# Giving every matmul operand the same place within 256 bytes, and the expert queries without transposes

## The chip, the cores and the metric

The kernel runs on one core of one Trainium2 chip. The metric is the device time of one execution in microseconds (us): the median of three runs, and one further execution taken by the hardware profiler, from which the rows below come. Lower is better.

## What is computed

Two transformer blocks follow each other on 256 tokens of width 2048, all in float32. The first has a retention layer (8 heads, 256 wide) and a latent attention layer, each between a modulated norm and a gated residual. The second has a mixed attention layer (16 "forgetting" heads, 16 "dilated" heads) and a layer of experts: each token scores 8 x 2 x 128 keys, takes the 16 best pairs of each head out of 128 x 128 experts, and sums the chosen experts.

```
def peer(x, w_query, sub_keys, expert_down, expert_up):
    q = (xt @ w_query).reshape(T, PEER_HEADS, 2, PEER_HALF)
    scores = jnp.einsum('thpc,hpnc->thpn', q, sub_keys)
    vals, idx = lax.top_k(scores, PEER_TOPK)
    ...
    u = jnp.take(expert_down, ec, axis=0)
    hdn = jax.nn.gelu(jnp.einsum('ted,td->te', u, xc))
    ...
    return jnp.einsum('te,ted->td', gc * hdn, vsel)
```

## The kernel before, in words

**Split products.** Every large product is made of three matmuls on operands that are split into a high and a low part (`split`, lines 171 to 173: ScalarE copies `raw` to `wh`, VectorE forms `wl = raw - wh`). A matmul has a stationary operand of 128 x 128, which TensorE loads (the rows PEld), and a moving one, which it streams past it, 256 to 512 columns. The load for the next matmul starts with the stream of the present one, so two reads of SBUF run beside each other: the stream of matmul n and the weights of matmul n+1.

**Three shapes** carry the time.

- *Tokens stationary, weights moving* (`proj_steps`, lines 243 to 245): the activations' columns (`hT`, `zT`, `mT`, `zT1`) are stationary, 512 columns of `wh` or `wl` move (384, 416 or 424 in the latent layer; 256 and 272 in the two blocks with the forget gates).
- *Weights stationary, tokens moving* (`turned_steps`, lines 271 to 273, for the retention's queries and keys; `hidden`, lines 1214 to 1216, for the experts' first product): 128 columns of `wh` or `wl` are stationary, the 256 tokens of `hT` move. The result has its dimensions on the partitions.
- *Experts' second product* (`up_steps`, lines 1294 to 1296): the gated hidden values `Wh`, `Wl` are stationary, 512 columns of `wh` or `wl` move.

**Places in SBUF.** Pools lie one behind the other, in the order in which they are opened, and tiles behind each other in a pool. Nothing rounds their addresses, so small tiles (`colv` 928 bytes, `mhalf` 32 bytes, ...) shift all that lies behind. Of the address in the built program, the remainder by 256 bytes (the "place" below) is the same for all buffers of a kind:

| operands of a matmul n and of the load for n+1 | stream at | weights at | stream minus weights, by 256 |
|---|---|---|---|
| `proj`, weights `hT`, `zT1` (512 columns) | 224 | 32 | 192 |
| `proj`, weights `mT` | 224 | 64 | 160 |
| `proj`, weights `zT` | 224 | 96 | 128 |
| `proj`, 424 columns, odd rows of the block | 128 | 32 | 96 |
| `proj`, 256 columns (forget block) | 224 | 32 | 192 |
| `turned`, `hidden` (256 columns) | 32 | 224 | 64 |
| `up` (512 columns) | 224 | 224 | 0 |

**The experts' queries** (`scores`, from line 1360): four blocks of 512 columns of `peer_query_2` go through `proj`, 96 matmuls of 512 columns each. Per block, ScalarE copies the two results out of PSUM with the factor `rtok` (line 1396); `tail` then, as a background task of the next block, transposes 2 x 4 squares of 128 x 128 (line 1374), copies them (1376), multiplies by the keys (1380) and copies the scores (1382). The scores feed `route`, the search for the best, mostly VectorE work, which runs beside the queries and the first experts.

**Order.** One program order per engine, made by the builder from the code's order and its pools; background tasks are interleaved by fixed rates (`later`, `tick`). SP issues all weight transfers in that order. The constants `cst` (identity, ones, masks, tables) come by one DMA at the start and stay.

Of the kernel before, what the change touches and what calls it, by code (L numbers as in the profile page):

```python
# [32 lines left out]
HB = 4  # L33
ADA_RATE = 0.3


C_ID, C_ONE, C_TRI, C_IOTA, C_CAUSAL, C_DIL, C_COS2, C_SIN2, C_INVF, C_COLF, C_END = (
    0, 128, 256, 384, 512, 768, 1152, 1168, 1184, 1216, 1224)
# [86 lines left out]
class Net:  # L125
    def __init__(self, ctx, tc, a):
        self.ctx, self.tc, self.nc, self.a = ctx, tc, tc.nc, a
        self.keep = ctx.enter_context(tc.tile_pool(name="keep", bufs=1))
        self.st = ctx.enter_context(tc.tile_pool(name="stream", bufs=1))
        self.sm = ctx.enter_context(tc.tile_pool(name="small", bufs=1))  # L130
        self.dr = ctx.enter_context(tc.tile_pool(name="dram", bufs=1, space=bass.MemoryType.DRAM))
        self.ps = ctx.enter_context(tc.tile_pool(name="psum", bufs=1, space=PSUM))
        self.bg = []
        self.nhalf, self.extra = 0, None
        self.places = places()
# [39 lines left out]
    def weights(self, name, k, c0):  # L175
# [5 lines left out]
        for j in range(2):  # L181
            wh, wl = self.halves()
# [75 lines left out]
    def turned_steps(self, ps, hT, nk, name, c0):  # L258
# [4 lines left out]
        for k0 in range(hT[0], hT[0] + nk, 4):  # L263
            for wh, wl in self.weights(name, k0, c0):
# [122 lines left out]
    def start(self):  # L387
        nc, keep, a = self.nc, self.keep, self.a
        self.ident = keep.tile([128, 128], F32, name="ident")
        self.colv = keep.tile([128, V_END], F32, name="colv")  # L390
        nc.scalar.dma_start(self.colv, a["vectors"])
        nc.sync.dma_start(self.ident, a["consts"][:, C_ID:C_ID + 128])
        self.cst = keep.tile([128, C_END], F32, name="cst")
# [4 lines left out]
        self.mhalf = keep.tile([128, 8], F32, name="mhalf")  # L398
        nc.vector.memset(self.mhalf, -0.5)

        self.cact = keep.tile([128, 16], F32, name="cact")
# [7 lines left out]
        nc.scalar.dma_start(self.cst, a["consts"])  # L409
# [3 lines left out]
    def angles(self, pool):  # L413
# [5 lines left out]
        self.cos = keep.tile([128, 2, 32], F32, name="cos")  # L419
        self.sin = keep.tile([128, 2, 32], F32, name="sin")  # L420
# [8 lines left out]
        pi = keep.tile([128, 2], I32, name="posi")  # L429
        nc.scalar.dma_start(pi, pos.rearrange("o (b p) -> p (o b)", p=128))  # L430
        pf = keep.tile([128, 2], F32, name="posf")
# [146 lines left out]
    def retention(self):  # L578
# [3 lines left out]
        self.A1 = keep.tile([128, 16], F32, name="A1")  # L582
        self.B1 = keep.tile([128, 16], F32, name="B1")
        with self.phase("ret", 8), self.tc.tile_pool(name="ret", bufs=1) as pool:
            A = pool.tile([128, 16], F32, name="A0")
            B = pool.tile([128, 16], F32, name="B0")
# [195 lines left out]
    def latent(self):  # L782
        nc, a = self.nc, self.a
        w_in, w_out, w_uq, w_ukv = "mla_w_in", "mla_w_out", "mla_w_uq", "mla_w_ukv"
        causal = self.cst[:, C_CAUSAL:C_CAUSAL + 256]
        scale = float(192 ** -0.5)
        with self.phase("mla", 7), ExitStack() as es:
            pool = es.enter_context(self.tc.tile_pool(name="mla", bufs=1))
            G = pool.tile([128, D], F32, name="G1")
            front = ExitStack()  # L790
# [4 lines left out]
            ss = pool.tile([128, 4], F32, name="latss")  # L795
# [16 lines left out]
            def latents():  # L812

                lr = pool.tile([128, 4], F32, name="latr")
# [126 lines left out]
            fa = self.keep.tile([128, 16], F32, name="fa")  # L941
# [6 lines left out]
            self.rtok = self.keep.tile([128, 2], F32, name="rtok")  # L948
# [25 lines left out]
    def mixed(self):  # L974
        nc, a = self.nc, self.a
        w_in, w_out = "w_in_2", "w_out_2"
        causal = self.cst[:, C_CAUSAL:C_CAUSAL + 256]
        with self.phase("mix", 8), self.tc.tile_pool(name="mix", bufs=1) as pool:
            hT, rtok = self.hT, self.rtok
            next(self.norms)  # L980
            norms = self.later(self.norms, 0.9)
            trig = pool.tile([128, 2, 2, 8], F32, name="trig")
# [3 lines left out]
            lf = pool.tile([128, 2, 16], F32, name="lf")  # L986
# [20 lines left out]
            cum = pool.tile([128, 2, 16], F32, name="cum")  # L1007
# [12 lines left out]
            def project(n, g, beside=iter(())):  # L1020
# [17 lines left out]
                for off in (0, 1024):  # L1038
                    def ev(tb, p, off=off):
# [5 lines left out]
                        dst = pool.tile([128, 1, 8, 66], F32, name="qk2", bufs=2)  # L1045
# [26 lines left out]
            def head(n, g, h):  # L1072
# [3 lines left out]
                else:  # L1076
                    mask = lambda tb: self.cst[:, C_DIL:C_DIL + 128] if tb == 0 else \
                        self.cst[:, C_DIL + 128:C_DIL + 384]
# [14 lines left out]
            def finish(n):  # L1093
# [7 lines left out]
                r = pool.tile([128, 2], F32, name=f"r_{n}")  # L1101
# [38 lines left out]
            self.rtok = self.keep.tile([128, 2], F32, name="rtok2")  # L1140
# [3 lines left out]
    def peer(self):  # L1144
# [5 lines left out]
        with self.phase("peer", 4), self.tc.tile_pool(name="peer", bufs=1) as pool:  # L1150
# [30 lines left out]
            def fetch(e):  # L1181
# [4 lines left out]
                for half in range(2):  # L1186
                    dh, dl = self.halves()
# [173 lines left out]
    def scores(self, qp, rp, hT, slots, normed, fetch):  # L1361
# [8 lines left out]
        def tail(b, qn):  # L1370
            for tb in range(2):
                p2 = self.tmp()
                for j in range(4):
                    nc.tensor.transpose(p2[:, j * 128:j * 128 + 128], qn[tb][:, j * 128:j * 128 + 128], self.ident)
                qT = qn[tb]
                nc.scalar.activation(qT, p2, AF.Copy)
                yield
                p3 = self.tmp()
                for j in range(4):
                    nc.tensor.matmul(p3[:, j * 128:j * 128 + 128], qT[:, j * 128:j * 128 + 128], kT[:, b * 4 + j, :],  # L1380
                                     start=True, stop=True)
                nc.scalar.activation(sc[tb][:, b * 4:b * 4 + 4, :].rearrange("p k n -> p (k n)"), p3, AF.Copy)
# [8 lines left out]
        for b in range(4):  # L1391
            qn = []

            def ev(tb, p, qn=qn):
                qn.append(self.w())
                nc.scalar.activation(qn[tb], p, AF.Copy, scale=self.rtok[:, tb:tb + 1])
# [12 lines left out]
        return steps, tail(3, qn)  # L1409
# [215 lines left out]
```

## Time and profile before

| | us |
|---|---|
| median of the runs (lowest, highest) | 3252.47 (3251.17, 3254.47) |
| the profiled execution: its own time | 3252.83 |
| its span, first to last instruction | 3251.0 |
| TensorE busy | 3159.2 (97%) |
| weight loads (PEld) busy | 2762.0 (85%) |
| VectorE busy | 2366.0 (73%) |
| ScalarE, GpSimd busy | 1558.4, 414.4 |

The profiled execution's own time is 1.8 us more than its span, and 0.4 us more than the median. A matmul's row shows its full passage (a 512-column one about 390 ns), and passages overlap; what one adds to the time is the distance from its start to the start of the next. The timeline lists the starts to 0.01 us.

### The profile page before, as it was taken

What the parts mean: (1) busy time and instruction counts of PE and PEld (TensorE: products, weight loads), DVE (VectorE), ACT (ScalarE), POOL (GpSimd) and SP (SyncE); (2) the same over time, 40 slices, a digit from 0 to 9 for tenths busy, and PEclk for the clock granted to TensorE, in tenths of its full rate; (3) what the DMA queues carried; (4) which work ended last, traced back from release to release, by engine and by line L of the source; (5) the groups of instructions that cost most, each with busy time, mean ns of one, the idle gap of its engine ahead of it and who ended that gap; (6) DMA issues with size and microseconds to landing.
All of it is one profiled execution on the core that took longest, in us unless ns stands there. A gap on an engine that the chain in (4) does not pass through costs nothing.

```text
span 3251.0 us, 47605 instructions
## 1 busy us (share of the span) xinstructions
PE 3159.2 (97%) x18562; PEld 2762.0 (85%) x18562; DVE 2366.0 (73%) x3918; ACT 1558.4 (48%) x2162; POOL 414.4 (13%) x487
## 2 busy tenths in 40 slices
PE   4999999999999999999999999999999999999998
PEld 4888977887798888888888999999888898999987
DVE  6898878878787675455669966998766656556665
ACT  3444434344545455555554444555444444444444
POOL 0001210201000320000000312886000000000000
PEclk9999999999999999999999999999999999999999
DMA  8875677786585435444454456777966755555554
GB/s 342 305 268 203 244 270 296 254 300 243 202 289 201 143 130 196 144 153 145 143 185 152 158 198 212 260 242 258 314 238 235 239 201 207 196 202 186 194 194 142
DMA packets 141681, 705.68 MB, mean 217 GB/s; under 512 B 12680, under 2 KB 45832, under 8 KB 67728
## 3 DMA queue, kind: packets, MB, share of 16 engines
q1 hardware_dynamic: 139152, 696.51, 60.9%
q10 hardware_dynamic: 2304, 6.14, 0.5%
q8 instruction: 145, 2.38, 0.3%
q14 instruction: 80, 0.66, 0.1%
HBM read 676.38 MB, written 26.21 MB: 216 GB/s over the span
## 4 chain that ended last, share of the span: by engine, by line
PE 83%; DVE 8%; DMA 4%; issue 3%; ACT 1%; POOL 0%; SPq 0%; DVEq 0%; POOLq 0%; ACTq 0%
PE acc L244 11%; PE acc L245 11%; PE acc L243 11%; PE acc L1294 7%; PE acc L1296 7%; PE acc L1295 7%; PE tmp L1214 5%; PE tmp L1216 5%; PE tmp L1215 5%; DVE wl L173 3%; PE acc L272 2%; PE acc L273 2%; PE acc L271 2%; PE tmp L359 1%; PE acc L1214 1%
## 5 line engine op out<-in xcount | busy, mean ns | idle before, releaser
L173 DVE TENSOR_TENSOR wl<-raw,wh 128x1024 fp32r<-128x1024 f32 (+4 forms) x983 | 1197.2, 1225 | 469.9 <-ACT wh L172 467.6
L172 ACT ACTIVATE wh<-raw 128x1024 fp32r<-128x1024 f32 (+4 forms) x983 | 1018.3, 1044 | 1017.9 <-PE acc L245 343.6
L244 PE MATMUL acc<-wl,hTh 128*128 128x512 f32 (+4 forms) x1280 | 497.4, 389 | 13.1 <-DVE wl L173 13.1
L243 PE MATMUL acc<-wh,hTh 128*128 128x512 f32 (+4 forms) x1280 | 498.3, 391 | 1.5 <-ACT wh L172 1.5
L245 PE MATMUL acc<-wh,hTl 128*128 128x512 f32 (+4 forms) x1280 | 496.7, 388 | 0.0
L1214 PE MATMUL tmp<-hTh,wh 128*128 128x256 f32 x1280 | 361.5, 282 | 0.0
L1216 PE MATMUL tmp<-hTl,wh 128*128 128x256 f32 x1280 | 357.6, 279 | 0.0
L1215 PE MATMUL tmp<-hTh,wl 128*128 128x256 f32 x1280 | 357.5, 279 | 0.0
L1294 PE MATMUL acc<-wh,Wh 128*128 128x512 f32 x812 | 317.4, 391 | 2.8 <-ACT Wh L172 1.5
L1296 PE MATMUL acc<-wh,Wl 128*128 128x512 f32 x812 | 316.5, 390 | 0.9 <-DVE Wl L173 0.9
L1295 PE MATMUL acc<-wl,Wh 128*128 128x512 f32 x812 | 316.3, 390 | 0.0
L244 PEld LDWEIGHTS acc<-wl,hTh 128*128 128x128 f32 x1280 | 241.8, 189 | 63.1 <-DVE wl L173 18.4
L245 PEld LDWEIGHTS acc<-wh,hTl 128*128 128x128 f32 x1280 | 241.8, 189 | 47.9 <-DVE hTl L310 0.4
L243 PEld LDWEIGHTS acc<-wh,hTh 128*128 128x128 f32 x1280 | 241.2, 189 | 46.5 <-ACT wh L172 1.7
L1214 PEld LDWEIGHTS tmp<-hTh,wh 128*128 128x128 f32 x1280 | 240.4, 188 | 0.7
L1216 PEld LDWEIGHTS tmp<-hTl,wh 128*128 128x128 f32 x1280 | 240.9, 188 | 0.1
L1215 PEld LDWEIGHTS tmp<-hTh,wl 128*128 128x128 f32 x1280 | 239.7, 187 | 0.8
L1512 POOL TENSOR_SCALAR oh<-iota,slot 128x128 f16<-128x128 f16 x256 | 208.6, 831 | 168.6 <-DVE iota L1503 87.0
L471 DVE SCALAR_TENSOR_TENSOR w<-raw,cact,w 128x512 f32<-128x512 f32 x240 | 186.9, 779 | 23.1 <-DMA raw<-in_ada_dram 18.5
L1215 PE MATMUL acc<-hTh,wl 128*128 128x256 f32 x640 | 179.9, 281 | 6.9 <-DVE wl L173 6.9
L162 POOL TENSOR_TENSOR tiny<-tiny,mhalf 128x1 f32<-128x1 f32 (+1 forms) x23 | 18.8, 819 | 1303.6 <-DVE tiny L161 1303.6
L1294 PEld LDWEIGHTS acc<-wh,Wh 128*128 128x128 f32 x812 | 152.4, 188 | 36.5 <-DVE x L1303 2.9
(370 smaller groups left out, 5919.8 us busy)
## 6 DMA issues: line engine op xcount, KB each, us to landing
raw<-in_down_dram SPq DMA_DIRECT2D x128, 1024.0 KB, 5.0
raw<-in_up_dram SPq DMA_DIRECT2D x128, 1024.0 KB, 5.0
raw<-in_ret_w_in_dram SPq DMA_DIRECT2D x96, 1024.0 KB, 6.0
raw<-in_ada_dram SPq DMA_DIRECT2D x64, 1024.0 KB, 4.9
raw<-in_w_in_dram SPq DMA_DIRECT2D x44, 1024.0 KB, 4.9
raw<-in_ret_w_out_dram SPq DMA_DIRECT2D x32, 1024.0 KB, 4.9
G<-in_ada_first_dram SPq DMA_DIRECT2D x32, 512.0 KB, 5.8
raw<-in_mla_w_out_dram SPq DMA_DIRECT2D x16, 1024.0 KB, 4.9
```

The costliest lines, as they stand in the source:

```text
L172: self.nc.scalar.activation(h, raw, AF.Copy)
L173: self.nc.vector.tensor_tensor(l, raw, h.bitcast(F32), op=OP.subtract)
L243: nc.tensor.matmul(o, sh, wh[:, j, :], start=(k == 0), stop=False)
L244: nc.tensor.matmul(o, sh, wl[:, j, :], start=False, stop=False)
L245: nc.tensor.matmul(o, sl, wh[:, j, :], start=False, stop=(k == nk - 1))
L1214: nc.tensor.matmul(o, dh[:, s], hh[:, k % 4, :], start=(k == 0), stop=False)
L1215: nc.tensor.matmul(o, dl[:, s], hh[:, k % 4, :], start=False, stop=False)
L1216: nc.tensor.matmul(o, dh[:, s], hl[:, k % 4, :], start=False, stop=(k == 15))
L1294: nc.tensor.matmul(y[tb][c], Wh[:, s], uh[:, u], start=first, stop=False)
L1295: nc.tensor.matmul(y[tb][c], Wh[:, s], ul[:, u], start=False, stop=False)
L1296: nc.tensor.matmul(y[tb][c], Wl[:, s], uh[:, u], start=False, stop=last)
L1512: nc.gpsimd.tensor_scalar(oh2[:, t, :], iota, k2, None, op0=OP.is_equal)
```

## The change

All tiles that are matmul operands are put at one place: small tiles go to a pool `little` of their own, behind which a pad makes all later pools begin at 128 (by 256 bytes), and odd-sized tiles are rounded up or cut out of it. The constants are reordered; the masks and the identity leave `cst` and are loaded by their layers, the causal mask by `latent`, both masks by `mixed`, through ScalarE's DMA queue. `wh` and `wl` get 64 columns more, and where they serve as stationary weights (`turned_steps`, the experts' `fetch`) they are used from column 16 on, 64 bytes behind. The table becomes:

| operands | stream at | weights at | stream minus weights, by 256 |
|---|---|---|---|
| `proj`, all of 512, 384, 256 columns | 128 | 128 | 0 |
| `proj`, 424 columns, odd rows | 32 | 128 | 160 |
| `turned`, `hidden` | 128 | 192 | 192 |
| `up` | 128 | 128 | 0 |

The experts' queries go through `turned_steps`: 192 matmuls of 256 columns for each block in the place of 96 of 512. They come out with their dimensions on the partitions, so `tail` has no transposes and no copies of them; the factor `rtok` moves to the copy of the scores.

```diff
+PAD = 56
+SHIFT = 16
...
+        self.little = ctx.enter_context(tc.tile_pool(name="little", bufs=1))
+        self.little.tile([128, PAD], F32, name="pad")
...
-    def halves(self):
+    def halves(self, still=False):
...
-            return tuple(self.extra.tile([128, 1024], F32R, name=n, bufs=1) for n in ("xh", "xl"))
-        return tuple(self.st.tile([128, 1024], F32R, name=n, bufs=HB) for n in ("wh", "wl"))
+            t = [self.extra.tile([128, 1088], F32R, name=n, bufs=1) for n in ("xh", "xl")]
+        else:
+            t = [self.st.tile([128, 1088], F32R, name=n, bufs=HB) for n in ("wh", "wl")]
+        o = SHIFT if still else 0
+        return tuple(x[:, o:o + 1024] for x in t)
...
-            for wh, wl in self.weights(name, k0, c0):
+            for wh, wl in self.weights(name, k0, c0, True):
...
-        self.colv = keep.tile([128, V_END], F32, name="colv")
+        self.colv = self.little.tile([128, V_END], F32, name="colv")
...
-        self.cst = keep.tile([128, C_END], F32, name="cst")
+        self.cst = self.little.tile([128, C_CAUSAL], F32, name="cst")
...
-        nc.scalar.dma_start(self.cst, a["consts"])
+        nc.scalar.dma_start(self.cst, a["consts"][:, :C_CAUSAL])
...
+            causal = pool.tile([128, 256], F32, name="causal")
+            nc.scalar.dma_start(causal, a["consts"][:, C_CAUSAL:C_CAUSAL + 256])
...
+            masks = pool.tile([128, 640], F32, name="masks")
+            nc.scalar.dma_start(masks, a["consts"][:, C_CAUSAL:C_CAUSAL + 640])
...
-            fb = pool.tile([128, 16], F32, name="fb")
+            fb = self.little.tile([128, 16], F32, name="fb")
...
-                    dh, dl = self.halves()
+                    dh, dl = self.halves(True)
...
-        def tail(b, qn):
+        def tail(b, qT):
+            yield
             for tb in range(2):
-                p2 = self.tmp()
+                p = self.tmp()
                 for j in range(4):
-                    nc.tensor.transpose(p2[:, j * 128:j * 128 + 128], qn[tb][:, j * 128:j * 128 + 128], self.ident)
-                qT = qn[tb]
-                nc.scalar.activation(qT, p2, AF.Copy)
-                yield
-                p3 = self.tmp()
-                for j in range(4):
-                    nc.tensor.matmul(p3[:, j * 128:j * 128 + 128], qT[:, j * 128:j * 128 + 128], kT[:, b * 4 + j, :],
+                    o = j % 2 * 256 + tb * 128
+                    nc.tensor.matmul(p[:, j * 128:j * 128 + 128], qT[j // 2][:, o:o + 128], kT[:, b * 4 + j, :],
                                      start=True, stop=True)
-                nc.scalar.activation(sc[tb][:, b * 4:b * 4 + 4, :].rearrange("p k n -> p (k n)"), p3, AF.Copy)
+                nc.scalar.activation(sc[tb][:, b * 4:b * 4 + 4, :].rearrange("p k n -> p (k n)"), p, AF.Copy,
+                                     scale=self.rtok[:, tb:tb + 1])
                 yield
...
-            self.proj(hT, 0, 16, "peer_query_2", b * 512, 512, ev)
+            ps = [self.acc() for _ in range(2)]
+            for _ in self.turned_steps(ps, (0, hT), 16, "peer_query_2", b * 512):
+                self.tick()
+            qT = []
+            for p in ps:
+                qT.append(self.w())
+                nc.scalar.activation(qT[-1], p, AF.Copy)
             if b < 3:
-                self.later(tail(b, qn), 1.0)
+                self.later(tail(b, qT), 1.0)
```

Outside the queries the order of the matmuls is the same, instruction by instruction. Where it moves:

TensorE in the query blocks, before: between two rounds of the block's matmuls (three lines, `hT` stationary) stand four transposes of the block before, one round of weights later its four products with the keys.

```order
L244 MATMUL acc<-wl,hTh_14393 128x512
L245 MATMUL acc<-wh,hTl_14394 128x512
L1374 MATMUL tmp<-ident,w 128x128 x4
L243 MATMUL acc<-wh,hTh_14393 128x512
L244 MATMUL acc<-wl,hTh_14393 128x512
...
L245 MATMUL acc<-wh,hTl_14394 128x512
L1380 MATMUL tmp<-keysT,w 128x128 x4
L243 MATMUL acc<-wh,hTh_14489 128x512
```

The same place after the change: the rounds are twice as many and half as wide, and only the products with the keys stand between them.

```order
L281 MATMUL acc<-hTl_14402,wh 128x256
L282 MATMUL acc<-hTh_14401,wl 128x256
L1387 MATMUL tmp<-keysT,w 128x128 x4
L280 MATMUL acc<-hTh_14497,wh 128x256
L281 MATMUL acc<-hTl_14498,wh 128x256
L282 MATMUL acc<-hTh_14497,wl 128x256
```

The 32 transposes and their copies are gone; the 32 products with the keys stay.

SP at the end of the latent layer, before, with what each transfer waits for: the forget bias `fb` lies in a pool that opens there and waits for VectorE and GpSimd to leave the memory, with weight transfers behind it.

```order
L179 DMA raw<-in_w_in_dram 128x1632 [waits DMAHW7_49,DVE_49,Activation_49]
L984 DMA fb<-in_forget_bias_dram 128x16 [waits DVE_49,Pool_49]
L179 DMA raw<-in_w_in_dram 128x1632 [waits DMAHW0_49,DVE_49,Activation_49]
L179 DMA raw<-in_w_in_dram 128x1088 [waits DMAHW1_49,DVE_49]
L179 DMA raw<-in_w_in_dram 128x2048 [waits DMAHW2_49,DVE_49]
```

Now `fb` is in `little`, and its transfer stands far ahead, among the first layer's weights, and waits for nothing:

```order
L188 DMA raw<-in_ret_w_in_dram 128x2048 [waits DMAHW2_49,DVE_49]
L188 DMA raw<-in_ret_w_in_dram 128x2048 [waits DMAHW7_49,DMAHW3_49,DVE_49]
L996 DMA fb<-in_forget_bias_dram 128x16
L188 DMA raw<-in_ret_w_in_dram 128x2048 [waits DMAHW5_49,DVE_49]
```

Only that one transfer has moved on SP.

ScalarE at the same place after the change: the transfer of both masks, which was not there before, stands ahead of those of the norm's gains and waits for VectorE, as the first of those did and does.

```order
L323 ACTIVATE hTh_10634<-tmp,fa 128x256 [waits PE_49] x2
L990 DMA masks<-in_consts_dram 128x640 [waits DVE_49]
L967 DMA w<-in_final_norm_g_dram 128x512 [waits DVE_49,Activation_49,Pool_49]
L323 ACTIVATE hTh_10634<-tmp,fa 128x256 [waits DVE_49] x2
L323 ACTIVATE hTh_10654<-tmp,fa 128x256 [waits PE_49] x2
```

The copies behind it come in the same order as before.

## Rows read from the trace of the kernel before

**Rows 1.** The page: busy time of each engine, and the chain that ended last

```profile
PE 3159.2 (97%) x18562; PEld 2762.0 (85%) x18562; DVE 2366.0 (73%) x3918; ACT 1558.4 (48%) x2162; POOL 414.4 (13%) x487
PE 83%; DVE 8%; DMA 4%; issue 3%; ACT 1%; POOL 0%; SPq 0%; DVEq 0%; POOLq 0%; ACTq 0%
```

**Rows 2.** Timeline of TensorE (start, duration, line): `proj`, places 192 apart, 192 matmuls

```profile
243.38 0.40 PE L243 MATMUL acc<-wh,hTh 128*128 128x512 f32 x1
...
288.19 0.28 PE L271 MATMUL acc<-hTh,wh 128*128 128x256 f32 x1
```

**Rows 3.** The same: `up`, places 0 apart, 192 matmuls

```profile
2291.54 0.39 PE L1294 MATMUL acc<-wh,Wh 128*128 128x512 f32 x1
...
2335.09 0.46 PE L1294 MATMUL acc<-xh,Wh 128*128 128x512 f32 x1
```

**Rows 4.** The same: `proj`, places 128 apart, 135 matmuls

```profile
809.54 0.40 PE L245 MATMUL acc<-wh,sg 128*128 128x512 f32 x1
...
840.92 0.39 PE L245 MATMUL acc<-wh,sg 128*128 128x512 f32 x1
```

**Rows 5.** Instructions by line, shapes apart (count, busy us, mean ns, idle before)

```profile
L244 PE MATMUL acc<-wl,hTh 128*128 128x512 f32 x1056 | 422.0, 400 | 9.7 <-DVE wl L173 9.7
L1214 PE MATMUL tmp<-hTh,wh 128*128 128x256 f32 x1280 | 361.5, 282 | 0.0
```

**Rows 6.** Timeline of TensorE: `hidden`, places 64 apart, 676 matmuls

```profile
1886.31 0.28 PE L1216 MATMUL acc<-hTl,wh 128*128 128x256 f32 x1
...
1965.93 0.38 PE L1490 MATMUL tmp<-ident,pick 128*128 128x128 f32 x2
```

**Rows 7.** The same, at the same places, after a wait: 70 matmuls

```profile
1854.38 0.28 PE L1216 MATMUL acc<-hTl,wh 128*128 128x256 f32 x1
...
1862.32 0.28 PE L1214 MATMUL acc<-hTh,wh 128*128 128x256 f32 x1
```

**Rows 8.** The forget block, 256 columns, places 192 apart: 6, 61 and 8 matmuls

```profile
1222.85 0.28 PE L244 MATMUL acc<-wl,hTh 128*128 128x256 f32 x1
...
1223.53 0.27 PE L295 MATMUL tmp<-ident,x 128*128 128x128 f32 x1
...
1224.89 0.28 PE L245 MATMUL acc<-wh,hTl 128*128 128x256 f32 x1
...
1232.08 0.65 PE L243 MATMUL acc<-wh,hTh 128*128 128x256 f32 x4
...
1235.97 0.28 PE L245 MATMUL acc<-wh,hTl 128*128 128x256 f32 x1
...
1236.89 0.28 PE L245 MATMUL acc<-wh,hTl 128*128 128x256 f32 x1
```

**Rows 9.** By stage: stretch, us, then PE, PEld, DVE, ACT, POOL busy, clock, DMA, GB/s

```profile
1640.00:1738.00 98.00, 98.00 (x462) 80.19 (x461) 76.19 (x216) 49.31 (x73) 5.25 (x7) 1.00 0.49 174
1738.00:1890.00 152.00, 141.46 (x1068) 133.48 (x1068) 148.57 (x387) 65.98 (x82) 42.63 (x42) 0.99 0.46 159
2050.00:2255.00 205.00, 205.00 (x1946) 203.87 (x1945) 197.53 (x507) 110.84 (x148) 164.65 (x204) 1.00 0.74 247
```

**Rows 10.** Timeline of TensorE in the queries: four transposes between rounds

```profile
1690.99 0.60 PE L1374 MATMUL tmp<-ident,w 128*128 128x128 f32 x4
1691.34 0.48 PE L243 MATMUL acc<-wh,hTh 128*128 128x512 f32 x1
1691.66 0.39 PE L244 MATMUL acc<-wl,hTh 128*128 128x512 f32 x1
```

**Rows 11.** Timeline of TensorE, 424 columns: five 96 apart, then six 192 apart

```profile
911.53 0.36 PE L244 MATMUL acc<-wl,hTh 128*128 128x424 f32 x1
...
912.51 0.36 PE L243 MATMUL acc<-wh,hTh 128*128 128x424 f32 x1
...
913.64 0.36 PE L243 MATMUL acc<-wh,hTh 128*128 128x424 f32 x1
```

**Rows 12.** Who SP's queue waited for, 1195 to 1245 us

```profile
SPq L984 <- DVE w L560: 3.2, 1, 3.2
```

**Rows 13.** Timeline of TensorE in the gates: 16 float16 matmuls of 128 columns

```profile
2084.81 1.07 PE L1530 MATMUL acc<-oh,oh 128*128 128x128 f16 x16
2085.68 0.37 PE L1214 MATMUL tmp<-hTh,wh 128*128 128x256 f32 x1
```

More of the change, by code (lines that the diff above doesn't have):

```diff
@@ L173, in split, with weights @@
         self.nc.vector.tensor_tensor(l, raw, h.bitcast(F32), op=OP.subtract)
-    def weights(self, name, k, c0):
+    def weights(self, name, k, c0, still=False):
         pos, nk, n = self.places[name, k, c0]
@@ L181, in weights @@
         for j in range(2):
-            wh, wl = self.halves()
+            wh, wl = self.halves(still)
             self.split(raw[:, j * m:j * m + m], wh[:, :m], wl[:, :m])
@@ L418, in angles @@
         self.sinT = pool.tile([128, 256], F32, name="sinT")
-        self.cos = keep.tile([128, 2, 32], F32, name="cos")
-        self.sin = keep.tile([128, 2, 32], F32, name="sin")
+        self.cos = self.little.tile([128, 2, 32], F32, name="cos")
+        self.sin = self.little.tile([128, 2, 32], F32, name="sin")
         pos = a["positions"]
@@ L428, in angles @@
         nc.vector.tensor_copy(self.onesr, self.ones)
-        pi = keep.tile([128, 2], I32, name="posi")
+        pi = self.little.tile([128, 2], I32, name="posi")
         nc.scalar.dma_start(pi, pos.rearrange("o (b p) -> p (o b)", p=128))
-        pf = keep.tile([128, 2], F32, name="posf")
+        pf = self.little.tile([128, 2], F32, name="posf")
         nc.vector.tensor_copy(pf, pi)
@@ L794, in latent @@
             lat = {}
-            ss = pool.tile([128, 4], F32, name="latss")
+            ss = self.little.tile([128, 4], F32, name="latss")
             for n, c0 in (("q", 0), ("kv", 512)):
@@ L812, in latents @@
             def latents():
-                lr = pool.tile([128, 4], F32, name="latr")
+                lr = self.little.tile([128, 4], F32, name="latr")
                 self.rsqrt(lr, ss, 1.0 / 512, 4)
@@ L938, in latent @@
             self.done(beside)
-            fa = self.keep.tile([128, 16], F32, name="fa")
+            fa = self.little.tile([128, 16], F32, name="fa")
             nc.vector.tensor_tensor(fa, self.colv[:, V_FN:V_FN + 16], self.colv[:, V_AT:V_AT + 16], op=OP.mult)
@@ L947, in latent @@
             next(cols)
-            self.rtok = self.keep.tile([128, 2], F32, name="rtok")
+            self.rtok = self.little.tile([128, 2], F32, name="rtok")
             self.norms = self.renorm(ss)
@@ L1006, in ev_forget @@
                 nc.vector.scalar_tensor_tensor(lf[:, tb, :], f, 0.0, ln, op0=OP.min, op1=OP.subtract)
-            cum = pool.tile([128, 2, 16], F32, name="cum")
+            cum = self.little.tile([128, 2, 16], F32, name="cum")
             def forget():
@@ L1076, in head @@
                 else:
-                    mask = lambda tb: self.cst[:, C_DIL:C_DIL + 128] if tb == 0 else \
-                        self.cst[:, C_DIL + 128:C_DIL + 384]
+                    mask = lambda tb: dil[:, 0:128] if tb == 0 else dil[:, 128:384]
                 def done(o, rd):
@@ L1100, in finish @@
                 nc.vector.tensor_reduce(s2, ss.rearrange("p (b c) -> p b c", b=2), axis=AX.X, op=OP.add)
-                r = pool.tile([128, 2], F32, name=f"r_{n}")
+                r = self.little.tile([128, 2], F32, name=f"r_{n}")
                 self.rsqrt(r, s2, 1.0 / 1024, 2)
@@ L1139, in mixed @@
             self.squares(ss, 3)
-            self.rtok = self.keep.tile([128, 2], F32, name="rtok2")
+            self.rtok = self.little.tile([128, 2], F32, name="rtok2")
             nc.vector.tensor_copy(self.rtok, self.rstd(ss))
@@ L1391, in scores @@
         for b in range(4):
[L1392 to L1396, printed above, removed]
             if b == 1:
```

27 lines of the change are left out of this document (13 added, 14 removed).

## The prediction

> **What bounds the kernel now.** I read the page first. TensorE is busy 97% of the span and holds 83% of the chain that ended last [rows 1]: a gain must come out of TensorE's own stream, and work taken from other engines gains nothing by itself. Next the view by stages: the granted clock is 0.99 to 1.00 wherever TensorE streams [rows 9], its upper level of 2.4 GHz, so no clock is to be won. A 512-column matmul has a mean of 400 ns in the view by line, and a 256-column one 282 [rows 5], but these are passages that overlap. So I went to the timeline and counted starts over stretches without a pause:
>
> - 512 columns: stream and next weights 192 apart 44.81 us / 192 = 233.4 ns [rows 2]; 128 apart 31.38 / 135 = 232.4 [rows 4]; 0 apart 43.55 / 192 = 226.8 [rows 3].
> - 256 columns, 64 apart: 79.62 / 676 = 117.8 ns [rows 6]; the same line, at the same places, keeps 7.94 / 70 = 113.4 in another stretch [rows 7]. A spacing, once taken, lasts from one wait to the next; over the trace, 6 of 99 runs without a wait have the short one.
> - 256 columns, 192 apart, which only the forget block has: 0.68 / 6 = 113, 7.19 / 61 = 117.9, 0.92 / 8 = 115 [rows 8]. A fourth run, of 10, lies at 115. The short spacing comes in three of four.
> - 424 columns: 96 apart 0.98 / 5 = 196 ns, 192 apart 1.13 / 6 = 188 [rows 11].
>
> The short spacings agree: 226.8 / 512 and 113.4 / 256 are both 0.443 ns per column, the others 0.455 to 0.460. I read the excess as a collision of the two reads of SBUF, which depends on how far apart their places lie.
>
> **The change, part by part.** Counts are from the program's order. The sum is made against the profiled execution's own time, 3252.8 us, which lies 0.4 above the median.
>
> *A. 512 columns, to 0 apart.* Lines 243 to 245 have 1632 matmuls each of this width; the queries take 128 of each away, 3 x 1504 = 4512 stay. Each goes from 233.4 to 226.8 or 226.9, so 6.4 to 6.6: 28.9 us. `up` is at 0 already and gains nothing. About 6% stand behind a wait, which swallows the gain of what precedes it, and behind VectorE in two layers it may slip a little more: I take **-26**. Bounds: nothing (if the reason is another, below) and -30.
>
> *B. 256 columns, 64 to 192 apart.* `turned` and `hidden` issue 1536 + 6144 = 7680. Bounds for one: 117.8 (no gain) and 113.4 (-4.4). The nearest rows are those at 192 apart [rows 8], short in three of four; 0.75 x 4.4 = 3.3. Not all of it reaches the end: from 1738 to 1890 VectorE is busy 148.57 of 152 us (the search for the best) and TensorE waits, with 141.46 busy [rows 9], so the 922 matmuls there gain nothing; from 2050 to 2255 VectorE has 197.53 of 205 [rows 9] and half of some 1530 count. 7680 - 922 - 765 = 5990, by 3.3: **-20**. Bounds 0 and -26.
>
> *C. The queries.* 384 x 233.4 = 89.6 us become 768 x 114.5 = 87.9 (90.5 at 117.8). Thirty-two transposes go: a group of four takes from 1690.99 to 1691.34, and the next matmul's successor starts 0.32 after it where 0.23 is usual [rows 10], so 0.35 + 0.09, by 8 groups: 3.5. The products with the keys stay. Together -5.2 at most. The copies that fall away are ScalarE's, busy 49 of 98 there [rows 9], and cost nothing now. VectorE's share is 76.19 of 98 in this stretch, but it fills up at its end, and `route` then bounds what follows: scores that come earlier are worth something only as far as `route` can start earlier. I take **-3.5**; bounds -6 and +1.
>
> *D. Other widths.* The 424-column matmuls move from 96 and 192 apart by rows to 160 and 0. No row shows 160 at this width; 188 and 196 are the neighbours. The 384-column ones go to 0. **-1**, bounds -1.5 and +0.4.
>
> *E. Moved transfers.* `fb` moves past many weight transfers on SP and no longer waits; the 3.2 us that SP stood behind VectorE for it [rows 12] stalled TensorE by at most 1, as weights were loaded ahead. The masks and the causal mask are now asked for on ScalarE's queue; they wait for VectorE as the gain's transfer behind them did, so no copy behind them is held longer, and they are needed only some products later. At the start the constants are shorter. Each of these moves a wait that others cover; if the masks' cover goes, one transfer's time of about 2 us is paid. **0**, bounds -2 and +2.
>
> Sum: -26 - 20 - 3.5 - 1 = -50.5, so **3202**.
>
> **A rule that speaks against A and B.** The row shows 226.8 at 0 apart and 233.4 at 192 [rows 2, 3]. The Trainium skill, "TensorE: Matmul & The Clock Gate", Part 2, step 1 of "Step-by-step", says that TensorE has two independent read ports in SBUF, and that loading the next weights steals no read bandwidth from the running matmul. By that rule, places would be worth nothing and A and B would be 0; the trace speaks against it, but only if the place is what differs between the two rows. This is the second rival.
>
> **The rivals.**
>
> *R1: the 256-column matmuls stay at 117.8.* For it: the longest run at 192 apart, 61 matmuls, is at 117.9 [rows 8], and 512 columns at 192 apart are slow [rows 2]. Against it: the three short ones, and [rows 7]. Then B is 0 and C is 90.5 - 89.6 - 3.5 = -2.6, taken as -1.5: -26 - 1.5 - 1 = -28.5, **3224**.
>
> *R2: the place is not what matters,* and the change doesn't do what it says. `up` differs from `proj` in more than places: its weights are `Wh` and `Wl`. Then 226.8 is a trait of `up`, and C alone remains: +0.9 - 3.5, and less of it behind VectorE: **3251**. Against it: [rows 6, 7] show two spacings for one line, and 424 columns change spacing with the row of the block alone [rows 11].
>
> *R3: slower; weights 64 bytes behind the stream collide harder.* 424 columns have 196 at 96 apart against 188 at 192 [rows 11], a factor of 1.043; at 192 no 512-column row is better than 128 or 160. Were 256 columns hit by the same factor at their new place, 117.8 would become 122.9, and 7680 x 5.1 = +39; the queries' 768 x 122.9 = 94.4 against 89.6, less 3.5, makes +1.3; A and D still give -27: **3266**. It decides from 117.8 + 29.6 / (7680 + 768) = about 121.3 ns on, where 29.6 is what A, C and D save at 117.8. Against it: no 256-column row lies above 117.9.
>
> *R4: all of the excess is collision,* and all goes. Sixteen float16 matmuls of 128 columns take 0.87 us [rows 13], 0.425 ns per column, that is 217.5 and 108.8: 4512 x 15.9 = 72, 5990 x 9 = 54, `up` 3072 x 9.3 = 29 and the queries some 7: **3091**. Against it: `up` is at 0 apart already and has 226.8. The same page of the Trainium skill ("Back-to-back issue gap") gives N / 2.4 GHz + 2.5 ns, 216 for 512 columns; no float32 row here reaches it.
>
> **How the numbers follow.** Chances: forecast 0.60, own range 3190 to 3214 (A from -22 to -29, B from -12 to -26, C to E by their bounds, not all at one end); R1 0.24, 3216 to 3232; R2 0.07; R3 0.06; R4 0.03. The range of 8 in 10 takes in the forecast's and most of R1's: **3188 to 3230**. A measurement of this kernel can tell about 0.2%, 6.5 us, from no change. Forecast, R1 and R4 are faster by more, 0.87; R2 lies within 0.2%, 0.07, and with a mild R3, 0.08; slower 0.05.
>
> **What would show it.** In the timeline of the changed kernel: `proj` at 226 to 227 ns by start (A right) or at 233 (R2); `hidden` at 113 to 115 in most stretches (B right), 117.8 (R1), 121 and more (R3); neither width below 0.44 ns per column (else R4). By line: no transposes in `tail`, and no idle time ahead of the products with the keys. In the stages: the queries' stretch 3 to 6 us shorter, the search's 152 us unchanged with VectorE still near 149, and all other stages of 256 and 512 columns shorter by 3 to 4%. At the start, SP's wait for `fb` gone and none in its place behind the masks. I am wrong if the spacing shortens and the end does not move: then VectorE or the transfers were closer behind TensorE than its 97% shows.

## The result, and the profile after

The changed kernel takes 3223.72 us in the median (3221.17 to 3234.75, five runs) against 3252.47 before: a ratio of 0.9922, 95% interval 0.9902 to 0.9941. In a later series it had 3226.01 (3219.57 to 3229.08). That is inside the range, but 22 us above the forecast (3202) and outside the forecast's own range (3190 to 3214); it is where the first rival stood (3224).

The page of the changed kernel, which answers to [rows 1]:

```profile
PE 3125.9 (97%) x18914; PEld 2769.7 (86%) x18914; DVE 2368.1 (74%) x3918; ACT 1553.4 (48%) x2154; POOL 415.0 (13%) x487
PE 61%; DVE 7%; DMA 3%; issue 1%; ACT 1%; POOL 0%; DVEq 0%; POOLq 0%; SPq 0%; ACTq 0%
```

TensorE still bounds the kernel. It is busy 33.3 us less in a span that is 29.1 us shorter, although it has 352 matmuls more. The shares of its chain add up to 73%, since the page follows it back only to about 890 us; the 61% is not to be set against the 83% of before.

The timeline of its TensorE over the same stretches as [rows 2] and [rows 3], 192 matmuls each:

```profile
239.10 0.40 PE L252 MATMUL acc<-wh,hTh 128*128 128x512 f32 x1
...
282.65 0.28 PE L280 MATMUL acc<-hTh,wh 128*128 128x256 f32 x1
...
2263.66 0.39 PE L1305 MATMUL acc<-wh,Wh 128*128 128x512 f32 x1
...
2307.21 0.46 PE L1305 MATMUL acc<-xh,Wh 128*128 128x512 f32 x1
```

`proj` now has 43.55 / 192 = 226.8 ns where it had 233.4; the experts' second product stays at 226.8. The 512-column spacing came as predicted.

The same view for 256 columns. The first two rows bound 724 matmuls in the stage of [rows 6], the next two a group of 96 behind the experts' second product, the last two 190 matmuls ahead of it:

```profile
1858.28 0.28 PE L1227 MATMUL acc<-hTl,wh 128*128 128x256 f32 x1
...
1940.36 0.38 PE L1499 MATMUL tmp<-ident,pick 128*128 128x128 f32 x2
...
2585.70 0.28 PE L1225 MATMUL tmp<-hTh,wh 128*128 128x256 f32 x1
...
2597.01 0.40 PE L1305 MATMUL acc<-wh,Wh 128*128 128x512 f32 x1
...
2237.80 0.28 PE L1226 MATMUL tmp<-hTh,wl 128*128 128x256 f32 x1
...
2260.17 0.28 PE L1227 MATMUL tmp<-hTl,wh 128*128 128x256 f32 x1
```

82.08 / 724 = 113.4 ns, but 11.31 / 96 = 117.8 and 22.37 / 190 = 117.7. All three are 192 apart. Over the whole trace 2652 of 8544 matmuls of this width start the next one within 115.5 ns (the "short" ones below); before it was 290 of 7776.

**Where the 29 us came from.** Outside the queries both programs have the same matmuls in the same order, so the distance from each start to the next can be subtracted pair by pair, for these two traces; the times of the stretches are those of the trace before. "Streaming" are the matmuls without a pause in either trace.

| part | gain, us | predicted |
|---|---|---|
| start: first matmul 4.7 earlier, waits of the small matmuls behind it 4.7 longer | 0.0 | 0 |
| 512 columns ahead of the queries: 4137 streaming, 233.0 to 227.7 ns, +21.9; 391 with a pause in one trace, -2.6 | 19.3 | 26 |
| 256 columns ahead of the queries (`turned`) | 2.5 | B, 20 in all |
| other widths (272 to 424) | 1.4 | 1 |
| the queries, 1665 to 1777 us | 0.1 | 3.5 |
| `hidden`, 1777 to 1879: +2.5 streaming, -2.7 in waits | -0.2 | 0, part of B |
| `hidden`, 1879 to 2039 | 4.4 | part of B |
| `hidden`, from 2039 on, beside the gates and between the second products | 0.5 | part of B |
| experts' second product | 1.2 | 0 |
| sum | 29.2 | 50.5 |

The stretch of the queries, and below it a part of it, by the view of windows (after the length come PE, PEld, DVE, ACT and POOL busy, then the clock):

```profile
1642.02:1754.12 112.10, 106.22 (x885) 105.74 (x883) 97.05 (x280) 51.86 (x64) 9.10 (x10) 0.97 0.47 167
...
1720.00:1730.00 10.00, 7.90 (x65) 7.41 (x63) 9.46 (x28) 4.44 (x6) 0.62 (x1) 1.00 0.27 89
1730.00:1740.00 10.00, 6.23 (x31) 6.23 (x32) 9.62 (x24) 2.74 (x3) 2.60 (x1) 0.66 0.62 216
```

And the timeline of TensorE there:

```profile
1733.77 0.58 PE L282 MATMUL acc<-hTh,wl 128*128 128x256 f32 x1 [3.89 <-DVE wl L182]
1734.15 0.42 PE L280 MATMUL acc<-hTh,wh 128*128 128x256 f32 x1
...
1739.28 0.37 PE L280 MATMUL acc<-hTh,wh 128*128 128x256 f32 x1
1739.48 0.28 PE L281 MATMUL acc<-hTl,wh 128*128 128x256 f32 x1
```

TensorE runs ahead, waits 3.89 us for VectorE's split, and comes back at a lower granted clock: 0.66 in that slice, and 24 matmuls from 1734.15 to 1739.28, 214 ns each, which is 256 columns at 1.2 GHz. VectorE has 9.46 and 9.62 of 10 us. Before the change the same place had a wait of 3.00 us and seven 512-column matmuls at 427 ns; both costs grew. In this execution the stretch is as long as before (112.1 and 112.2 us).

### The profile page after: what moved, and what is told of

The parts are those of the page before. It is cut to its first block, busy times and chain, and to the rows that moved or that the text cites. A ratio compares the mean times of both kernels' runs of the same rounds, so it can differ in the third digit from the quotient of the medians.

```text
span 3221.9 us, 48304 instructions
## 1 busy us (share of the span) xinstructions
PE 3125.9 (97%) x18914; PEld 2769.7 (86%) x18914; DVE 2368.1 (74%) x3918; ACT 1553.4 (48%) x2154; POOL 415.0 (13%) x487
## 4 chain that ended last, share of the span: by engine, by line
PE 61%; DVE 7%; DMA 3%; issue 1%; ACT 1%; POOL 0%; DVEq 0%; POOLq 0%; SPq 0%; ACTq 0%
PE acc L1305 7%; PE acc L1306 7%; PE acc L1307 7%; PE acc L252 5%; PE acc L254 5%; PE acc L253 5%; PE tmp L1225 5%; PE tmp L1227 5%; PE tmp L1226 5%; DVE wl L182 3%; PE tmp L368 1%; PE acc L1226 1%; PE acc L1225 1%; PE acc L1227 1%; DMA raw<-in_mla_w_in_dram 1%; PE acc L1539 1%
## 5 line engine op out<-in xcount | busy, mean ns | idle before, releaser
L253 PE MATMUL acc<-wl,hTh 128*128 128x512 f32 (+4 forms) x1152 | 441.2, 383 | 9.1 <-DVE wl L182 9.1
L252 PE MATMUL acc<-wh,hTh 128*128 128x512 f32 (+4 forms) x1152 | 441.7, 386 | 1.5 <-ACT wh L181 1.5
L254 PE MATMUL acc<-wh,hTl 128*128 128x512 f32 (+4 forms) x1152 | 441.1, 383 | 0.0
L253 PEld LDWEIGHTS acc<-wl,hTh 128*128 128x128 f32 x1152 | 217.2, 189 | 48.4 <-DVE wl L182 13.7
L254 PEld LDWEIGHTS acc<-wh,hTl 128*128 128x128 f32 x1152 | 217.2, 189 | 36.5 <-DVE hTl L319 0.4
L252 PEld LDWEIGHTS acc<-wh,hTh 128*128 128x128 f32 x1152 | 216.9, 189 | 36.2 <-ACT wh L181 1.7
L282 PE MATMUL acc<-hTh,wl 128*128 128x256 f32 x768 | 217.2, 283 | 5.9 <-DVE wl L182 5.9
L280 PE MATMUL acc<-hTh,wh 128*128 128x256 f32 x768 | 220.6, 288 | 0.1
L281 PE MATMUL acc<-hTl,wh 128*128 128x256 f32 x768 | 216.9, 283 | 1.6 <-DVE hTl L319 1.6
L480 DVE SCALAR_TENSOR_TENSOR w<-raw,cact,w 128x512 f32<-128x512 f32 x240 | 186.2, 776 | 27.3 <-DMA raw<-in_ada_dram 22.6
```

The costliest lines, as they stand in the source:

```text
L252: nc.tensor.matmul(o, sh, wh[:, j, :], start=(k == 0), stop=False)
L253: nc.tensor.matmul(o, sh, wl[:, j, :], start=False, stop=False)
L254: nc.tensor.matmul(o, sl, wh[:, j, :], start=False, stop=(k == nk - 1))
L280: nc.tensor.matmul(o, sh, hh, start=(k == 0 and c % 2 == 0), stop=False, skip_group_check=True)
```

## Experiments

My theory behind the result: (1) the distance between the stream's place and the next weights' place, by 256 bytes, sets the spacing; (2) at 256 columns the distance only says which spacings there are, and the moment at which a stretch starts, behind a wait or another kind of matmul, picks one. Rivals: the places play no part; the place itself counts, not the distance; the queries carry the gain; the spacing is picked at the start, whatever the place.

### The old queries at the new places

The edit takes back the part of the diff on `scores`:

```diff
-            for _ in self.turned_steps(ps, (0, hT), 16, "peer_query_2", b * 512):
-                self.tick()
+            self.proj(hT, 0, 16, "peer_query_2", b * 512, 512, ev)
...
+                    nc.tensor.transpose(p2[:, j * 128:j * 128 + 128], qn[tb][:, j * 128:j * 128 + 128], self.ident)
```

> The changed kernel with the queries of before: 96 matmuls of 512 columns per block, 32 transposes and their copies back. Places stay those of the change. Theory (the gain is the 512-column places; the queries gain nothing, because their 256-column matmuls keep 117.8 ns and VectorE's search ends the stretch): 3224, within 3 us of the changed kernel. Prediction's term C: 3.5 us longer, 3227. Rival (the queries carry most of the 29 us): 3240 or more.

Measured: 3227.36 (3224.49 to 3229.44), ratio 0.9921 (0.9904 to 0.9938). The layout alone has nearly all of the gain. Against 3223.72 and 3226.01 of the changed kernel, the queries are worth between 1 and 4 us, which is within the spread of the runs: theory and term C can't be told apart here, the rival falls.

### 256 columns back at 64 apart

```diff
-SHIFT = 16
+SHIFT = 48
```

> Stationary weights used 192 bytes behind the buffer's start in place of 64, so 256-column streams and weights lie 64 apart, as before the change; 512-column matmuls stay at 0 apart. Theory (at 192 apart about a third of the 256-column matmuls get 113.4 ns, at 64 apart some 3%): the 9.9 us that these gained are lost, some 3 us come back from VectorE's waits, so 3231, and under 5% of the 256-column matmuls at 113.4. Rival (the place plays no part at 256 columns, only the waits before): 3224 and about a third short.

Measured: 3231.98 (3229.06 to 3235.34), ratio 0.994 (0.9923 to 0.9957), and 75 of 8544 matmuls within 115.5 ns. By the time alone this is not clear of the changed kernel, whose interval (0.9902 to 0.9941) overlaps; the count is what shows it, 75 against 2652. As the theory says: the place has a part at 256 columns too.

### 256 columns at 0 apart

```diff
-SHIFT = 16
+SHIFT = 0
```

> Stationary weights at the buffer's start: 256-column streams and weights 0 apart. Theory (0 apart is good at 512 columns and bad at 256: the forget block after the change has 119.8 ns there): 8448 matmuls from a mean of 116.4 to 119.8, less the 1700 beside the search, +23, so 3247. Rival (0 apart is best for every width, since no two reads collide): all at 113.4, 3224 less 15 to 20 = 3206. Rival (places play no part): 3224.

Measured: 3246.36 (3241.29 to 3252.05), ratio 0.998 (0.997 to 0.9989). The stretch of 724 matmuls in its timeline:

```profile
1869.17 0.28 PE L1227 MATMUL acc<-hTl,wh 128*128 128x256 f32 x1
...
1956.06 0.38 PE L1499 MATMUL tmp<-ident,pick 128*128 128x128 f32 x2
```

86.89 / 724 = 120.0 ns against 113.4. The distance that is best at 512 columns is the worst of the three tried by themselves at 256 (0, 64, 192), and takes back 22.6 of the 28.8 us that the change brings. This edit moves nothing but the stationary weights. The Trainium skill ("TensorE: Matmul & The Clock Gate", Part 2, "Step-by-step") has two independent read ports and no bandwidth taken by the next load; by that the two times would be alike, and they are not.

### 512 columns at 64 apart

```diff
-        o = SHIFT if still else 0
+        o = SHIFT
```

> Moving weights used from 64 bytes behind the buffer's start too, so the 512-column streams of proj and of the experts' second product lie 64 apart from the next weights; 256 columns stay 192 apart. Theory (the place sets the 512-column spacing): proj back to about 233 ns and the second product from 226.9 to 233, (4512 + 3072) x 6.2 x 0.9 = +42, so 3266. Rival (the second product is short for a reason of its own, proj for its place): +25, 3249. Rival (places play no part): 3224.

Measured: 3231.18 (3223.74 to 3239.74), ratio 0.9932 (0.991 to 0.9953). I had missed by 35 us, and the timeline says twice why:

```profile
238.65 0.40 PE L252 MATMUL acc<-wh,hTh 128*128 128x512 f32 x1
...
282.62 0.28 PE L280 MATMUL acc<-hTh,wh 128*128 128x256 f32 x1
...
1651.07 0.28 PE L281 MATMUL acc<-hTl,wh 128*128 128x256 f32 x1
...
1673.98 0.60 PE L1172 MATMUL tmp<-ident,w 128*128 128x128 f32 x4
```

First, 64 apart is not as bad as 128 to 192: 43.97 / 192 = 229.0 ns; the second product, which had 226.8 ever since the kernel before, has 229 too, so its short spacing was one of place. Second, 202 matmuls of the queries, 22.91 / 202 = 113.4 ns, though their operands lie where they lie in the changed kernel, whose timeline has 117.8 for the same 202:

```profile
1642.25 0.28 PE L281 MATMUL acc<-hTl,wh 128*128 128x256 f32 x1
...
1666.04 0.61 PE L1172 MATMUL tmp<-ident,w 128*128 128x128 f32 x4
```

4702 of 8544 matmuls are within 115.5 ns here, against 2652. The places are the same: the first sign for part 2 of the theory. But it is not shown that the shifted streams ahead of the stretch made the difference. The run with short matmuls of 16 columns, further below, has the changed kernel's instructions at the changed kernel's places up to 2590 us, and its trace has the short spacing for the same 202 as well, 22.91 / 202 = 113.4:

```profile
1645.05 0.28 PE L281 MATMUL acc<-hTl,wh 128*128 128x256 f32 x1
...
1667.96 0.60 PE L1172 MATMUL tmp<-ident,w 128*128 128x128 f32 x4
```

So one and the same instruction stream takes either spacing, from one execution to the next.

### Everything moved by 96 bytes

```diff
+        self.keep.tile([128, 24], F32, name="lead")
```

> Every buffer moved up by 96 bytes (a tile of 96 bytes ahead of all): streams at 224 and tokens at 224 in place of 128, weights behind at 32; all differences stay. Theory (only stream minus next weights counts): 3224, within 3 us, 512 columns at 227 ns. Rival (the place itself counts, 128 being good and the 224 and 32 of before bad): 512 columns at 232 to 234, 4512 x 6 x 0.9 = +24, so 3248.

Measured: 3226.56 (3225.01 to 3229.13), ratio 0.9916 (0.9899 to 0.9932). The stretch of [rows 2] there:

```profile
239.40 0.40 PE L253 MATMUL acc<-wh,hTh 128*128 128x512 f32 x1
...
282.94 0.28 PE L281 MATMUL acc<-hTh,wh 128*128 128x256 f32 x1
```

43.54 / 192 = 226.8. The distance counts, not the place.

### Two maps

In the first the moving weights start by turns 0, 32, ... 256 bytes behind, in the second the stationary ones (the edit of the first is shown):

```diff
-        o = SHIFT if still else 0
+        o = SHIFT
+        if not still:
+            o = self.nmove // 2 % 9 * 8
+            self.nmove += 1
```

> A map, not a variant: the moving weights of proj and of the experts' second product start 0, 32, ... 256 bytes behind the buffer's start, by turns from one block of weights to the next, so one trace shows the 512-column spacing at each distance from the next weights. Theory (each distance has its spacing): 0 at 226.9, 64 at 229 (from the run with 64), 128 at 232.4, 160 at 234, 192 at 233.4, both for proj and for the second product. Rival (what was seen goes with the weights' kind or the stage): the same spacing at every distance within a stage. Time by the theory: a mean of some 231 over 7584 matmuls, +28, less up to 10 at 256 columns: 3242 to 3252.

> A map: the stationary weights of the 256-column matmuls start 0, 32, ... 256 bytes behind, by turns from one block of weights to the next, so one trace shows their spacing at each distance. Theory (the place gives the odds, the wait before picks): 0 at 119.8 always, 192 at 113.4 or 117.8 by stretch, 64 at 117.8 nearly always; the other distances unknown, some may be short more often. A rival (the spacing is picked at the wait and kept whatever the place behind it): no change of spacing from one block of weights to the next within a stretch. Time by the theory: 3220 to 3240.

Mean spacing in ns of matmuls without a pause; the 256 columns are those of `hidden` in the second map:

| stream minus weights | 0 | 32 | 64 | 96 | 128 | 160 | 192 | 224 |
|---|---|---|---|---|---|---|---|---|
| 512, `proj` | 227.8 | 233.2 | 229.4 | 233.6 | 232.7 | 234.0 | 233.2 | 233.0 |
| 512, second product | 227.3 | 233.3 | 229.7 | 233.7 | 232.8 | 234.1 | 233.3 | 233.1 |
| 424, `proj` | 192.8 | 191.9 | 193.3 | 195.8 | 194.5 | 191.5 | 187.9 | 193.1 |
| 256, `hidden` | 119.8 | 117.2 | 117.0 | 119.9 | 119.2 | 117.8 | 116.0 | 118.3 |

Measured 3246.1 (3243.74 to 3250.62), ratio 0.9981 (0.9968 to 0.9994), and 3233.75 (3231.63 to 3243.8), ratio 0.9946 (0.9926 to 0.9967). At 512 columns each distance has its spacing, the same in two stages and with other stationary operands; an offset of 256 bytes gives `proj` 227.8 as an offset of 0 gives 227.7, so the remainder by 256 is what counts. Each width has its own best distance: 0 at 512, 192 at 424 and, in this one execution, at 256. At 256 columns the spacing changes with the place within a stretch, so the start alone doesn't fix it; and the means there mix short and long matmuls (40% were short at 192 apart, 17% at 64, about 1% at 0), in shares that another execution may have otherwise.

### A short matmul ahead of a stretch

If the start picks the spacing, a matmul of a few columns should be able to change it. Ahead of each of the 22 groups between the second products:

```diff
                 o = hp[:, e % 2 * 256:e % 2 * 256 + 256]
+                if e % 2 == 0 and self.extra is not None:
+                    n0 = e // 2 % 8 * 8 + 8
+                    nc.tensor.matmul(o[:, :n0], both[0][0][:, 0:128], hT[0][0][:, 0, :n0], start=True, stop=True)
```

> Ahead of each group of 96 matmuls of 256 columns that follows the experts' second product, one short matmul of 8, 16, ... 64 columns (by turns) on the same operands, whose result the next one overwrites. If the spacing is picked by the moment at which the stretch starts: some of the widths turn the 96 behind them to 113.4, 0.42 us less for each group so turned, and the others stay at 117.8. Rival (after 512 columns at 0 apart the place alone makes it 117.8): all thirty groups stay at 117.8. The short matmuls cost some 0.1 us each, 3 us; time 3217 to 3224 by the first, 3227 by the rival.

Measured: 3218.53 (3216.04 to 3221.03, two runs), ratio 0.989 (0.987 to 0.9909). The group that took 11.31 us above:

```profile
2589.42 0.18 PE L1217 MATMUL tmp<-hTh,wh 128*128 128x24 f32 x1
2589.45 0.37 PE L1228 MATMUL tmp<-hTh,wh 128*128 128x256 f32 x1
2589.65 0.28 PE L1229 MATMUL tmp<-hTh,wl 128*128 128x256 f32 x1
...
2600.43 0.40 PE L1308 MATMUL acc<-wh,Wh 128*128 128x512 f32 x1
```

11.01 us, the short one and the long start behind it included; the matmuls after the first few have 113.3 ns, behind every one of the eight widths. Same line, same places, another start, another spacing: part 2 of the theory is shown for this place, in 22 groups of 22. (The 30 groups of my expectation were 22.)

### The same at 64 apart

```diff
-SHIFT = 16
+SHIFT = 48
```

> The short matmul of 16 columns ahead of each group behind the experts' second product, but with the stationary weights 192 bytes behind, so that 256-column streams and weights lie 64 apart, as before the change. If the start of a stretch alone picks the spacing: the 22 groups at 113.3, 7 us less than the run with 192 behind (3232), 3225. If the place must allow it too: they stay at 117.8, and the short matmuls cost 22 x 0.11 = 2.5: 3234.

Measured: 3232.3 (3229.0 to 3238.79), ratio 0.9933 (0.9917 to 0.995), no gain on the 3231.98 without the short matmul. A group:

```profile
2597.58 0.17 PE L1216 MATMUL tmp<-hTh,wh 128*128 128x16 f32 x1
2597.61 0.36 PE L1227 MATMUL tmp<-hTh,wh 128*128 128x256 f32 x1
...
2609.00 0.40 PE L1307 MATMUL acc<-wh,Wh 128*128 128x512 f32 x1
```

11.42 us: all 22 groups stay at 117.8, and the short matmul costs its 0.11. So the place must allow the short spacing, and the start must take it. At 64 apart it is not out of reach ([rows 7] had it), but this start doesn't find it.

### The faster versions

The changed kernel again, with a short matmul of 16 columns in each group, and with more of them: at the start of each block of `turned_steps`, and behind each step of the gates, there on zeros so that it adds nothing. Of the edits, the one in the gates (`again` is set behind a step):

```diff
+                    if again:
+                        n0 = e % 7 * 8 + 8
+                        nc.tensor.matmul(o[:, :n0], dh[:, s], self.pad[:, :n0], start=False, stop=False)
+                        again = False
```

> The changed kernel as it is, on one chip with the two that follow. 3224, within 3 us.

> The short matmul ahead of each group of 256-column matmuls behind the experts' second product, now 16 columns always. All such groups at 113.3 ns: about thirty groups, 96 x 4.4 = 0.42 less 0.11 for the short one and the bubble behind it, 0.3 us each: 7 to 9 us less than the changed kernel, 3215 to 3217. If the run with all widths was a lucky one: no difference.

> As the one before, and a short matmul also at the start of each block that has its dimensions on the partitions (the retention's queries and keys, the experts' queries), and, with zeros as its stream so that it adds nothing, behind each step of the gates (8, 16, ... 56 columns by turns). The four blocks behind 512 columns turn short: -1. In the gates' stretch some thirty runs of 59 matmuls: each that turns short gains 59 x 4.4 = 0.26 less 0.11, so -4 if all do and VectorE (197.5 of 205 us before) lets it through; +3.5 if none does. So 3211 to 3219, by the trace of the gates' stretch.

Measured on one chip: 3226.01 (3219.57 to 3229.08), ratio 0.9914 (0.99 to 0.9929); 3218.04 (3214.91 to 3224.35), ratio 0.9896 (0.9881 to 0.9911); 3216.57 (3215.65 to 3217.39), ratio 0.989 (0.9875 to 0.9906). The last kernel's runs all lie below the changed kernel's; the step between the two with short matmuls, 1.5 us, is within their spread.

The traces of the first two kernels show how much is left to the execution, for up to 2590 us their instructions are the same as those of the changed kernel's first trace. Short were, in that order (first trace, changed again, 16 columns): of the queries' 768 matmuls 68, 24 and 608; of the 791 of `hidden` that the table has as 1777 to 1879, 677, 218 and 180; of the 1322 behind them (1879 to 2039) 1175, 1174 and 456. The queries' stretch took 112.1, 111.5 and 110.1 us, the one of the 1322 took 155.6, 155.6 and 158.8 (160.0 before the change). So nothing in the program alone settles these starts. The groups of 96 between the second products were at 117.8 in both traces without the short matmul, and at 113.3 with it.

In the gates of the last one:

```profile
2033.71 0.28 PE L1550 MATMUL acc<-oh,oh 128*128 128x128 f16 x2
2033.80 0.27 PE L1234 MATMUL tmp<-pad,wh 128*128 128x56 f32 x1
...
2041.07 1.07 PE L1550 MATMUL acc<-oh,oh 128*128 128x128 f16 x16
2041.94 0.25 PE L1234 MATMUL tmp<-pad,wh 128*128 128x8 f32 x1
...
2048.95 0.84 PE L1550 MATMUL acc<-oh,oh 128*128 128x128 f16 x12
```

From the short matmul of 56 columns to the next, 2041.94 - 2033.80 = 8.14 us; with 8 to 48 columns the period is 7.88 in all steps but the first two, and without a short matmul it was 8.03. Behind 56 columns the matmuls stay at 118, behind the others they fall to 113 to 114. Here the width decides: the second matmul behind the 56 columns starts 205 ns after the first, behind the others 200. 6411 of 8544 matmuls are within 115.5 ns.

At the start of the blocks the short matmul worked both ways. In one of the retention's groups of 96 it ended a short spacing, 113.5 ns ahead of it and 117.9 behind:

```profile
359.69 0.28 PE L283 MATMUL acc<-hTl,wh 128*128 128x256 f32 x1
...
362.30 0.17 PE L281 MATMUL acc<-hTh,wh 128*128 128x16 f32 x1
362.33 0.36 PE L282 MATMUL acc<-hTh,wh 128*128 128x256 f32 x1
362.53 0.28 PE L283 MATMUL acc<-hTl,wh 128*128 128x256 f32 x1
...
370.78 0.28 PE L284 MATMUL acc<-hTh,wl 128*128 128x256 f32 x1
```

Against the first trace of the changed kernel, that group and one more fell from 92 and 91 short matmuls to 21 each; of the other five, three rose from 0 to 45, one from 0 to 92, and one had 72 for 77.

## Why the prediction was right, and where it was wrong

- **The number** held by the width of the range. The forecast's sum was 50.5 us and 29.2 came: A was 7 too high, B 13 and C 3; 1.2 of the second product and 0.4 of D make up the rest. The range took in 3224 only because it took in R1.
- **The bound** was right: TensorE stayed at 97%, and most of what its stream lost outside VectorE's stretches reached the end (19.3 of 21.9 us at 512 columns).
- **A** had the right premise, that the distance sets the spacing, and, with 226.8 for 233.4, the right spacing. The term was mis-sized: 19.3 in place of 26. I let 6% of the matmuls stand behind waits; 391 of 4528 had a pause in one of the traces, and there 2.6 us were given back. The streaming ones gained 5.3 ns each, not 6.4, since their mean after the change is 227.7, above the 226.8 of the unbroken stretch.
- **B failed**, at the step "the short spacing comes in three of four; 0.75 x 4.4". I read the odds from runs of 6, 8 and 10 matmuls and set aside the one run of 61 [rows 8], which was the better guide. I had the other half in hand ("a spacing, once taken, lasts from one wait to the next") and yet priced it as odds for each matmul. Where the starts repeat, the spacings did too: the groups behind the second product, and the runs beside the gates, started alike and came out alike, at 117.8. The short one was taken from 1777 to 2039 (up to 1879 without profit) and in parts of `turned`, in all about 7 us of the 20. And even that is one draw: the stretch from 1879 to 2039, which gave 4.4 of the 7 in both traces of the changed kernel, gave 1.2 in the trace of the run with 16 columns, by the same instructions. Odds were a fair way to price such a start, but per start and not per matmul.
- **The VectorE exception in B was right**: from 1777 to 1879 the matmuls gained 2.5 us and the waits took 2.7 back.
- **C** was too high by the trace, 0.1 for 3.5; the wait for VectorE grew from 3.6 us in all to 5.9, and the granted clock behind it was 0.66 for a slice (0.88 and 0.95 in two slices before). In the run with 16 columns, where 608 of the 768 were short, the stretch was 2.1 us shorter than before. The run with the old queries leaves 1 to 4 us open.
- **D**: 1.4 for 1, but not by the reason given. At 424 columns 0 apart is worse than 192 ([rows 11], and the map: 192.8 and 187.9), and 160 better than 96; the two nearly cancel. The gain is that of the 384-column matmuls, most of it in pauses.
- **E**: nothing, as said. The first matmul came 4.7 us earlier (the shorter constants are a likely reason, not a shown one), and the wait for `ada` ahead of the second kind grew from 14.53 to 18.47 us. SP's wait for `fb` [rows 12] is gone, with no gain to be seen. The masks' transfer took 3.1 us, and nothing is seen waiting for it.
- **The rivals**: R1 named the time, 3224, and its reason (the run of 61) was mostly right, though a third of the matmuls did turn short; that its sum, 28.5, met the 29.2 is luck, since A's 26 in it was 7 too much and B's 0 was 7 too little. R2 falls with the maps and the run at 0 apart, R3 with R1's own numbers (no long run at 192 apart above 117.9); one of its supports was misread, for at 512 columns 192 apart (233.3) was better than 160 (234.0) in the trace before. R4 falls because no long stretch went below 113.3 or 226.7 ns.

What stays open: why a distance is good, what a start must hit, and what differs between two executions that take a start differently. The trace shows the starts of loads and streams, not the reads of SBUF; "two reads that collide" is my reading, not shown.

## What to carry to other kernels

When TensorE's stream is the bound, count start to start over stretches without a pause, by width and by the distance of the two operands' addresses; the durations of single matmuls hardly show it (0.28 us in the rows at 113.4 and at 117.8 ns). Map the distances in one run by letting the offset rotate, since no distance was good for all widths. And where a view shows one instruction at two spacings, ask what stood ahead of each stretch before giving odds: the groups that followed each other alike took one spacing throughout, and one small instruction could change it, for better or worse. A start that comes once may differ between executions, so one trace does not settle it.

## What I had not expected of the hardware

- At 512 columns 0 apart is best (226.8 ns; 232.7 to 234.1 at six of the other seven), and at 256 columns it is the worst but one (119.8; 119.9 at 96 apart, lowest 116.0 at 192).
- A spacing of 113.4 or 117.8 ns, once taken, lasted for 724 and for 202 matmuls, without a pause between. The same 202, by the same instructions at the same places, had 117.8 in one execution and 113.4 in another.
- A matmul of 8 to 64 columns, some 28 ns to the next start, changed the 95 matmuls behind it by 4.5 ns each in all 22 groups at 192 apart; one of 16 columns did so in none of 22 at 64 apart.
